# Moving part of VectorE's exponential onto GpSimd, beside chosen VectorE instructions, in a multi-query attention kernel

## Chip, cores and metric

The kernel runs on one core of a Trainium2 chip. The metric is the device time in microseconds (us); lower is better. PE is the matrix engine (PEld its weight loads), ACT the scalar engine, DVE the vector engine, POOL is GpSimd and SP the sync engine, which here only starts DMAs.

## The reference

```python
q: (8, 1024, 16, 64)   k, v: (8, 1024, 64)      # float32, one k and v for all 16 heads
scores  = q @ k.T / sqrt(64)                    # per batch and head, 1024 x 1024
weights = exp(scores - max); weights /= sum(weights)
out     = weights @ v
```

There are 8 x 16 x 1024 x 1024 = 134 million exponentials. They are the work that this kernel spreads over engines.

## The kernel before

Two heads form a pair; there are 64 pairs with 8 key tiles each, 512 "tiles" of 128 keys x 2 heads x 1024 queries. For each tile PE computes the scores in two halves (128 x 1024 values in PSUM each), and a weight tile in fp16 comes back from one of two engines:

- ACT computes exp directly: two ACTIVATEs of 128x1024 per tile.
- DVE takes some tiles by another road. It turns the score into the bits of an fp16 number (`z`, two instructions, one per half), cuts out the exponent (`e`), builds a mantissa (`m`), squares it and multiplies it by `z`. The sum of `e`, `z` and this product, each with its own scaled copy of v, is close to exp. So a DVE tile costs PE three value products where an ACT tile costs one.

```python
def exp_dve(t, c):                       # once per half of the tile; cut
    V.tensor_scalar(out=z[half c], in0=scores, scalar1=vscale, scalar2=..., op0=mult, op1=add)
    steps[t] = (                                                  # each on 128 x 2048
        lambda: V.tensor_scalar(out=e, in0=z, scalar1=0xFC00, op0=bitwise_and),
        lambda: V.tensor_scalar(out=m, in0=z, scalar1=1023, scalar2=14 << 10, and, or),
        lambda: V.tensor_tensor(out=m, in0=m, in1=m, op=mult),    # the square
        lambda: V.tensor_tensor(out=m, in0=z, in1=m, op=mult),    # the product
    )
```

A planner (`plan`) simulates PE, ACT and DVE with assumed durations before the kernel is built. It decides which tiles go to DVE and fixes the order of every instruction on every engine. Its constants, such as `ACT_P` (the assumed spacing of ACTIVATEs), are tuned. POOL only starts DMAs (loads of q and k). The accumulated output is normalised on DVE (`rec`, `norm`).

The softmax here doesn't subtract the row's maximum and nothing guards it: scores larger than these inputs give would overflow.

Of the kernel before, what the change touches and what calls it, by code (L numbers as in the profile page):

```python
# [10 lines left out]
FP16 = mybir.dt.float16  # L11
U16 = mybir.dt.uint16
EXP = mybir.ActivationFunctionType.Exp
ALU = mybir.AluOpType
ENG = mybir.EngineType

P = 128
ONE = 1024.0
C0 = 0.4578223016
TERMS = (1.0, 1.017578125, 0.66650390625)  # L20

ACT_P, ACT_L = 0.905, 1.19
QK_P, AV_B, AV_1, SWITCH, PE_L = 0.22, 0.0295, 0.02, 0.10, 0.49
MARGIN, WAIT = 0.285, 0.097
END, END_LAG = 4.686, 0.6
VEC = dict(z=1.13, rec=0.11, val=0.34)
NORM = 0.07, 0.067
STEPS = (0.6, 0.6, 1.13, 1.13)
VEC_L = 0.19
VEC_DEP = 0.12  # L30
BACKLOG, BACK_END = 7.741, 3.823
LAST, SPLIT, FIRST = 13, 6, 3
RAMP, VALS, COLD, WARM = 0.395, 3.0, 1, 0.0
BUSY = 20, 3, 5, 2
WBUFS = 23
ZBUFS = 6
LAG = 1.833
FAR = 1e9
BLOCKS = (0, 6, 10, 16)
STEP = 2  # L40

def follows(x, y):
    if y is None:
        return False
    if len(x) == 5:
        return len(y) == 5 and x[1] == "norm" and y[1] == "rec" and x[2:] == y[2:]
    if len(x) != 2 or len(y) != 2:
        return False
    if y[0] == "z":
        return x in ((y[1], 0), (y[1], 1))  # L50
    return x[0] == y[0] and (x[1], y[1]) in ((2, 1), (3, 2))

def plan(NP, NKT, HP=8):
# [8 lines left out]
    def emit(t, *op):  # L62
        ops.append((t, len(ops), op))

    pe = act = dve = 0.0
    mode = ""
    slot = [0.0] * 3
# [10 lines left out]
    p, g = 0, 0  # L78
    groups: list = []
    zs: list = []  # L80
    evs: list = []
    steps: list = []
    vals = [(VALS, 0, k) for k in range(len(TERMS))]
    vdone: dict = {}
    last = None
    while p < NP or groups:
        assert min(pe, dve) < 2e3
        if pe <= dve:
# [23 lines left out]
                units = [(t, c) for c in range(2) for t in range(nt, n)]  # L112
                nt = n
            if nt // NKT >= HP * nb - 3 and nb * HP < NP:
                vals += [(T, nb, k) for k in range(len(TERMS))]
                nb += 1
            cold = COLD if T < WARM else 1
            free = [s for s in range(3) if slot[s] <= T + (SWITCH if mode != "qk" else 0)]
# [88 lines left out]
                pe = max(min(nxt, default=0.0), T + 1e-3)  # L207
        else:
            T = dve
            z = [x for x in zs if x[0] <= T + 0.25]  # L210
            todo = [("ev", x) for x in evs if x[0] <= T]
            todo += [("val", x) for x in vals if x[0] <= T][:1]
# [4 lines left out]
            if z:  # L217
                x = z[0]
                zs.remove(x)
                r, s, u = x  # L220
                T = max(T, r)
                emit(T, "z", *u)
                dve = T + VEC["z"]
                slot[s] = dve + VEC_L
                if u[1] == 1:
                    steps += [(u[0], n) for n in range(len(STEPS))]
                    ready[u[0], 1, "v"] = dve + VEC_L
                last = ("z", u[0])
            elif what == "ev":
                evs.remove(x)  # L230
                emit(T + late, *x[1:])
                dve = T + late + vec(x[1], x[3])
                if x[1] == "rec":
                    evs.insert(0, (T, "norm", *x[2:]))
                else:
                    acc[x[4]] = dve + VEC_L
                last = x
            elif what == "val":
                vals.remove(x)
                emit(T, "val", *x[1:])  # L240
                dve = T + VEC["val"]
                vdone[x[1:]] = dve + VEC_L
                last = None
            elif what == "step":
                steps.remove(x)
                emit(T + late, "step", *x)
                dve = T + late + STEPS[x[1]]
                if x[1] in (0, len(STEPS) - 1):
                    ready[x[0], x[1] and len(TERMS) - 1, "v"] = dve + VEC_L
                last = x  # L250
            else:
                nxt = [x[0] for x in zs + evs + vals if x[0] > T] + [pe + 1e-6] * (pe > T)
                dve = max(min(nxt, default=0.0), T + 1e-3)
                last = None
    for x in evs:
# [6 lines left out]
def kernel(  # L262
# [47 lines left out]
    zs: dict = {}  # L310
    ms: dict = {}
    steps: dict = {}
    acc: dict = {}
    rec: dict = {}
    osb: dict = {}

    def load_k(b):
        st = kst.setdefault(b, {})
        st["k16"] = kvp.tile([P, NKT, 2, D], FP16, tag="k16", name=f"k16{b}")
        for r in range(2):  # L320
            nc.gpsimd.dma_start(  # L321
                out=st["k16"][:, :, r, :], in_=k[b].rearrange("(p c) d -> p c d", p=P)
            )
# [4 lines left out]
            st["vn"] = kvp.tile([P, NKT, D], FP32, tag="vn", bufs=1, name=f"vn{b}")  # L328
        nc.sync.dma_start(out=st["vn"], in_=v[b].rearrange("(p c) d -> p c d", p=P))

    def scale_v(b, k):
        kst[b]["v"] = vals[b % 2]
        nc.vector.tensor_scalar(  # L333
            out=vals[b % 2][k][:, :, 0:D], in0=kst[b]["vn"], scalar1=TERMS[k], scalar2=None,
            op0=ALU.mult)

# [117 lines left out]
    def exp_dve(t, c):  # L454
        name = f"{t}"
        if c == 0:
            zs[t] = dvp.tile([P, 2, S], U16, tag="z", bufs=ZBUFS, name=f"z{name}")
        z = zs[t]
        nc.vector.tensor_scalar(  # L459
            out=z[:, :, c * QC : (c + 1) * QC], in0=sc.pop((t, c)), scalar1=vscale,  # L460
            scalar2=(15 + math.log2(C0)) * ONE, op0=ALU.mult, op1=ALU.add,
        )
        if c == 0:
            return
        V = nc.vector
        m = ms[t] = dvp.tile([P, 2, S], FP16, tag="m", bufs=ZBUFS, name=f"m{name}")
        wt[t] = dvp.tile([P, 2, S], FP16, tag="e", bufs=ZBUFS, name=f"e{name}")
        steps[t] = (
            lambda: V.tensor_scalar(  # L469
                out=wt[t].bitcast(U16), in0=z, scalar1=0xFC00, scalar2=None,  # L470
                op0=ALU.bitwise_and),
            lambda: V.tensor_scalar(  # L472
                out=m.bitcast(U16), in0=z, scalar1=1023, scalar2=14 << 10,
                op0=ALU.bitwise_and, op1=ALU.bitwise_or),
            lambda: V.tensor_tensor(out=m, in0=m, in1=m, op=ALU.mult),  # L475
            lambda: V.tensor_tensor(out=m, in0=z.bitcast(FP16), in1=m, op=ALU.mult),  # L476
        )

    def value(p, grp, j, k, x, n, end, s):
        if n == 0:  # L480
# [16 lines left out]
    def reciprocal(p, grp):  # L497
        a = blocks(p, grp)
        rec[p, grp] = recp.tile([P, 8], FP32, tag="rec", name=f"rec{p}_{grp}")
        nc.vector.reciprocal(out=rec[p, grp][:, 0 : a.shape[1]], in_=a[:, :, D])  # L500

    def normalise(p, grp):
        b, hp = divmod(p, HP)
        a = blocks(p, grp)
        n = a.shape[1]
        if grp == 0:
            osb[p] = osbp.tile([P, NKT, 2 * D], FP32, tag="osb", name=f"osb{p}")
        o = osb[p]
        nc.vector.tensor_tensor(  # L509
            out=o.rearrange("p i (h d) -> p (i h) d", h=2)[:, BLOCKS[grp] : BLOCKS[grp + 1], :],  # L510
            in0=a[:, :, 0:D],
            in1=rec.pop((p, grp))[:, 0:n].unsqueeze(2).broadcast_to([P, n, D]),
            op=ALU.mult,
        )
        acc.pop((p, grp))
        if p == NP - 1:
            i0, i1 = BLOCKS[grp] // 2, BLOCKS[grp + 1] // 2
        elif grp == 2:
            i0, i1 = 0, NKT
        else:  # L520
            return
        (nc.scalar if p == NP - 1 and grp == 1 else nc.sync).dma_start(
            out=out[b, P * i0 : P * i1, 2 * hp : 2 * hp + 2, :].rearrange(
                "(c p) h d -> p c (h d)", p=P),
            in_=o[:, i0:i1, :],
        )

    begun = 0

    def begin(w):  # L530
        if w % 2 == 0:
            if w + 4 < NP:
                load_q(w + 4)
            if w + 2 < NP:
                trans_q(w + 2)
        b, hp = divmod(w, HP)
        if b + 1 < B:
            if hp == 2:
                load_k(b + 1)
            if hp == 4:  # L540
                load_v(b + 1)
            if hp == HP - 3:
                trans_k(b + 1)

    with tc.manual_schedule(engines={ENG.PE, ENG.Activation, ENG.DVE, ENG.Pool}):
# [7 lines left out]
        for _, _, (op, *args) in order:  # L553
            if op == "qk":
                if scores == 5:
                    turn_first(2)
                scores += 1
                while begun <= args[0] // NKT:
                    begin(begun)
                    begun += 1  # L560
                score(*args)
                if scores < 3:
                    busy(BUSY[3])
                if scores == 3:
                    turn_first(1)
            elif op == "act":
                exp_act(*args)
            elif op == "z":
                exp_dve(*args)
            elif op == "val":  # L570
                scale_v(*args)
            elif op == "step":
                steps[args[0]][args[1]]()
            elif op == "av":
                value(*args)
            elif op == "rec":
                reciprocal(*args[:2])
            else:
                normalise(*args[:2])

_INS = ['q', 'k', 'v']
_OUTS = [((8, 1024, 16, 64), 'float32')]
# [24 lines left out]
```

## Time and profile before

The median is 763.3 us (15 runs, 761.9 to 766.0). The page of the profiled run begins with the busy time of each engine and its number of instructions, and gives the chain of work that ended last:

```profile
span 761.6 us, 29604 instructions
PE 733.1 (96%) x13648; PEld 489.6 (64%) x13648; DVE 723.3 (95%) x1048; ACT 749.0 (98%) x816; POOL 43.6 (6%) x60
ACT 88%; PE 10%; DVE 1%; DMA 0%; issue 0%
```

Three engines are almost full. The chain goes through ACT for 88% of the span. The groups of instructions of the same page show what each one does (columns: line, engine, operation, output and input with shapes, count | total busy us, mean ns of one | idle time just before them and what ended it):

```profile
L448 ACT ACTIVATE w<-sc 128x1024 f16<-128x1024 f32 x814 | 747.1, 1323 | 4.3 <-PE sc L436 4.2
L459 DVE TENSOR_SCALAR z<-sc 128x1024 uint16<-128x1024 f32 x210 | 256.2, 1220 | 15.0 <-PE sc L436 12.2
L475 DVE TENSOR_TENSOR m<-m 128x2048 f16<-128x2048 f16 x105 | 126.9, 1209 | 0.1
L476 DVE TENSOR_TENSOR m<-z,m 128x2048 f16<-128x2048 f16 x105 | 126.4, 1204 | 0.0
L469 DVE TENSOR_SCALAR e<-z 128x2048 uint16<-128x2048 uint16 x105 | 72.8, 693 | 0.0
L472 DVE TENSOR_SCALAR m<-z 128x2048 uint16<-128x2048 uint16 x105 | 72.1, 686 | 0.0
L333 DVE TENSOR_SCALAR vals<-vn 128x512 f16<-128x512 f32 x24 | 9.1, 412 | 0.0
```

DVE holds 105 of the 512 tiles, ACT the other 407 (814 ACTIVATEs). ACTIVATEs overlap: a record lasts 1.32 us in the mean, but neighbours start 0.904 us apart at the least and 0.921 us in the mean. The train of 813 spacings lasts 748.6 us, so about 15 us of the time are outside it (start, tail, and what the span leaves out). ACT sat idle before scores for 4.2 us only.

The ends of the records: 804 of 813 ends follow the end before by 0.914 to 0.919 us, 0.917 in the middle.

### The profile page before, as it was taken

How to read it: one execution, taken by the hardware profiler on the slowest of the kernel's cores; microseconds unless marked ns; L12 is line 12 of the kernel's file. 1: busy time of each engine (PE TensorE's matmuls, PEld its weight loads, DVE VectorE, ACT ScalarE, POOL GpSimd, SP SyncE). 2: the span in 40 equal slices, each digit the busy share in tenths (PEclk: the TensorE clock that was granted, in tenths of full speed). 3: DMA queues.
4: the chain of work that ended last, by engine and by line, in shares of the span. 5: the costliest groups of instructions: out<-in, count | busy, mean ns of one | idle time of the engine just before them, and what ended most of it. 6: DMA issues, size and time to landing. Idle time of an engine off the chain costs nothing.

```text
span 761.6 us, 29604 instructions
## 1 busy us (share of the span) xinstructions
PE 733.1 (96%) x13648; PEld 489.6 (64%) x13648; DVE 723.3 (95%) x1048; ACT 749.0 (98%) x816; POOL 43.6 (6%) x60
## 2 busy tenths in 40 slices
PE   8899999999999999999999999999999999999997
PEld 5456566666666666666666666666665666666666
DVE  5999999999999999999999999999999999999982
ACT  6999999999999999999999999999999999999997
POOL 2100010000100001000010000100000000000000
PEclk8999999999999999999999999999999999999999
DMA  6973475354754538654585543746548545342313
GB/s 124 120 134 71 84 125 109 76 106 93 116 102 78 124 59 132 113 94 97 92 122 97 113 95 89 111 87 127 111 78 102 104 85 113 85 86 58 84 51 92
DMA packets 189980, 75.04 MB, mean 99 GB/s; under 512 B 90272, under 2 KB 188832, under 8 KB 189856
## 3 DMA queue, kind: packets, MB, share of 16 engines
q1 hardware_dynamic: 140544, 54.01, 31.4%
q0 software_dynamic: 47840, 18.35, 21.3%
q8 instruction: 106, 1.74, 0.9%
q10 hardware_dynamic: 1472, 0.79, 0.3%
q14 instruction: 18, 0.15, 0.1%
HBM read 39.58 MB, written 33.55 MB: 96 GB/s over the span
## 4 chain that ended last, share of the span: by engine, by line
ACT 88%; PE 10%; DVE 1%; DMA 0%; issue 0%
ACT w L448 88%; PE acc L487 6%; PE sc L436 4%; DMA kn<-in_k_dram 0%; DVE z L459 0%; PE busy L392 0%; PE kps L412 0%; DVE osb L509 0%; PE qps L423 0%; DVE k L407 0%; DVE qt L425 0%; DVE rec L500 0%
## 5 line engine op out<-in xcount | busy, mean ns | idle before, releaser
L448 ACT ACTIVATE w<-sc 128x1024 f16<-128x1024 f32 x814 | 747.1, 1323 | 4.3 <-PE sc L436 4.2
L436 PE MATMUL sc<-qt,k2t 64*128 64x512 f16 x2048 | 345.6, 384 | 21.6 <-ACT w L448 16.4
L487 PE MATMUL acc<-vals,w 128*128 128x65 f16 x6512 | 314.4, 194 | 0.2 <-DVE osb L509 0.2
L487 PEld LDWEIGHTS <-w 128*128 128x128 f16 x6512 | 241.0, 97 | 98.4 <-issue 97.4
L459 DVE TENSOR_SCALAR z<-sc 128x1024 uint16<-128x1024 f32 x210 | 256.2, 1220 | 15.0 <-PE sc L436 12.2
L436 PEld LDWEIGHTS <-k2t 64*128 64x128 f16 x2048 | 100.6, 93 | 96.6 <-issue 43.6
L475 DVE TENSOR_TENSOR m<-m 128x2048 f16<-128x2048 f16 x105 | 126.9, 1209 | 0.1
L476 DVE TENSOR_TENSOR m<-z,m 128x2048 f16<-128x2048 f16 x105 | 126.4, 1204 | 0.0
L487 PE MATMUL acc<-vals,e 128*128 128x65 f16 x1680 | 110.6, 194 | 0.6 <-DVE osb L509 0.6
L487 PE MATMUL acc<-vals,z 128*128 128x65 f16 x1680 | 109.9, 194 | 0.0
L487 PE MATMUL acc<-vals,m 128*128 128x65 f16 x1680 | 104.5, 194 | 0.4 <-issue 0.4
L509 DVE TENSOR_TENSOR osb<-acc,rec 128x384 f32<-128x384 f32 (+1 forms) x192 | 96.8, 506 | 0.4
L487 PEld LDWEIGHTS <-e 128*128 128x128 f16 x1680 | 74.1, 97 | 25.2 <-issue 23.3
L487 PEld LDWEIGHTS <-z 128*128 128x128 f16 x1680 | 74.1, 97 | 22.2 <-issue 22.2
L487 PEld LDWEIGHTS <-m 128*128 128x128 f16 x1680 | 71.7, 97 | 22.3 <-issue 21.6
L469 DVE TENSOR_SCALAR e<-z 128x2048 uint16<-128x2048 uint16 x105 | 72.8, 693 | 0.0
L472 DVE TENSOR_SCALAR m<-z 128x2048 uint16<-128x2048 uint16 x105 | 72.1, 686 | 0.0
L356 POOL DMA_DIRECT2D qn<-in_q_dram x32 | 29.1, 910 | 620.9 <-DMA qt<-qn 587.5
L500 DVE RECIPROCAL rec<-acc 128x6 f32<-128x6 f32 (+1 forms) x192 | 34.4, 181 | 12.5 <-PE acc L487 12.5
L321 POOL DMA_DIRECT2D k<-in_k_dram x14 | 13.0, 933 | 0.0
L333 DVE TENSOR_SCALAR vals<-vn 128x512 f16<-128x512 f32 x24 | 9.1, 412 | 0.0
L392 PE MATMUL busy<-ident 128*128 128x128 f16 x32 | 4.2, 303 | 1.6 <-POOL ident masks.py:199 1.6
(22 smaller groups left out, 13.7 us busy)
## 6 DMA issues: line engine op xcount, KB each, us to landing
out_dram<-osb SPq DMA_DIRECT2D x63, 512.0 KB, 3.4
qn<-in_q_dram POOLq DMA_DIRECT2D x31, 512.0 KB, 5.9
vn<-in_v_dram SPq DMA_DIRECT2D x8, 256.0 KB, 3.7
k<-in_k_dram POOLq DMA_DIRECT2D x14, 128.0 KB, 5.8
qf<-in_q_dram ACTq DMA_DIRECT2D x2, 256.0 KB, 3.7
qt<-qn SPq DMA_TRANSPOSE x32, 4.6
out_dram<-osb SPq DMA_DIRECT2D x2, 192.0 KB, 2.1
qn<-in_q_dram POOLq DMA_DIRECT2D x1, 256.0 KB, 5.3
```

Of the source, the lines that this page charges most:

```text
L321: nc.gpsimd.dma_start(out=st["k16"][:, :, r, :], in_=k[b].rearrange("(p c) d -> p c d", p=P))
L356: nc.gpsimd.dma_start(out=qn[ps[0]].rearrange("p (c r) x -> p c (r x)", r=len(ps)), in_=q[b, :, 2 * hp : 2 * hp + 2 * len(ps), :].rearrang ...
L436: nc.tensor.matmul(sc[t, c][:, h, :], kst[p // HP]["k2t"][64 * h : 64 * h + 64, j, :], qt[p][64 * h : 64 * h + 64, 4 * c : 4 * c + 4, :], ...
L448: ins = nc.scalar.activation(out=w, in_=sc.pop((t, c)), func=EXP, scale=ascale).ins
L459: nc.vector.tensor_scalar(out=z[:, :, c * QC : (c + 1) * QC], in0=sc.pop((t, c)), scalar1=vscale, scalar2=(15 + math.log2(C0)) * ONE, op0= ...
L469: lambda: V.tensor_scalar(out=wt[t].bitcast(U16), in0=z, scalar1=0xFC00, scalar2=None, op0=ALU.bitwise_and),
L472: lambda: V.tensor_scalar(out=m.bitcast(U16), in0=z, scalar1=1023, scalar2=14 << 10, op0=ALU.bitwise_and, op1=ALU.bitwise_or),
L475: lambda: V.tensor_tensor(out=m, in0=m, in1=m, op=ALU.mult),
L476: lambda: V.tensor_tensor(out=m, in0=z.bitcast(FP16), in1=m, op=ALU.mult),
L487: nc.tensor.matmul(acc[p, grp][:, o : o + D + 1], w[:, h, i * P : (i + 1) * P], kst[p // HP]["v"][k][:, j, 0 : D + 1], start=(n == 0 and y ...
L500: nc.vector.reciprocal(out=rec[p, grp][:, 0 : a.shape[1]], in_=a[:, :, D])
L509: nc.vector.tensor_tensor(out=o.rearrange("p i (h d) -> p (i h) d", h=2)[:, BLOCKS[grp] : BLOCKS[grp + 1], :], in0=a[:, :, 0:D], in1=rec.p ...
```

## The change

The intent is to relieve DVE, so that it can take more tiles and ACT fewer. Of the square, 896 of 2048 columns go to POOL in two pieces of 448, and so do 21 of the 24 scalings of v. POOL and DVE share SBUF ports, so each piece is placed in the plan beside a DVE instruction that reads PSUM (`z`, or `rec` for the scalings), with an extra dependence on the DVE instruction ahead of it. A piece that finds no such place within 9.1 us gets a gap of 0.7 us on DVE in the plan. DMA starts of POOL are held until after a piece. Many of the tuned constants changed too.

```diff
-ACT_P, ACT_L = 0.905, 1.19
+ACT_P, ACT_L = 0.917, 1.19
-MARGIN, WAIT = 0.285, 0.097
-END, END_LAG = 4.686, 0.6
+MARGIN, WAIT = 0.309, 0.061
+END, END_LAG = 8.479, 0.592
-STEPS = (0.6, 0.6, 1.13, 1.13)
+STEPS = (0.6, 0.6, 0.665, 1.13)
+PIECE, PIECE_T, PIECE_AGE, LATE = 448, 1.2, 9.124, 0.7
...                                                   (more constants)
+    def beside(t, age, kinds):                        # planner
+        x = next((x for x in pool if x[0] <= t - age and x[1] in kinds), None)
...
             elif z: ...
+                beside(T, 0.3, ("sq",))               # a square piece goes beside z
                 emit(T, "z", *u)
...
-            lambda: V.tensor_tensor(out=m, in0=m, in1=m, op=ALU.mult),
+            lambda: square(V, 0, 2 * S - 2 * PIECE),
...
+    def beside(op, t, n):                             # building the kernel
+        if op == "sq":
+            a = 2 * S - (2 - n) * PIECE
+            ins = squares[t](nc.gpsimd, a, a + PIECE)
+        else:
+            ins = scale_v(t, n, nc.gpsimd)
+        (before, y), (last, x) = past[-2:]
+        tc.add_manual_dep(ins.ins, (last if follows(x, y) else before).name, ...,
+            reason="shared SBUF ports")
+        while later:
+            later.pop(0)()                            # DMA starts that were held back
```

The built kernel has 110 DVE tiles, 804 ACTIVATEs and 160 more value matmuls (11,712 for 11,552).

More of the change, by code (lines that the diff above doesn't have):

```diff
@@ L20 @@
 TERMS = (1.0, 1.017578125, 0.66650390625)
-ACT_P, ACT_L = 0.905, 1.19
+ACT_P, ACT_L = 0.917, 1.19
 QK_P, AV_B, AV_1, SWITCH, PE_L = 0.22, 0.0295, 0.02, 0.10, 0.49
-MARGIN, WAIT = 0.285, 0.097
-END, END_LAG = 4.686, 0.6
+MARGIN, WAIT = 0.309, 0.061
+END, END_LAG = 8.479, 0.592
 VEC = dict(z=1.13, rec=0.11, val=0.34)
 NORM = 0.07, 0.067
-STEPS = (0.6, 0.6, 1.13, 1.13)
+STEPS = (0.6, 0.6, 0.665, 1.13)
+PIECE, PIECE_T, PIECE_AGE, LATE = 448, 1.2, 9.124, 0.7
 VEC_L = 0.19
 VEC_DEP = 0.12
-BACKLOG, BACK_END = 7.741, 3.823
-LAST, SPLIT, FIRST = 13, 6, 3
-RAMP, VALS, COLD, WARM = 0.395, 3.0, 1, 0.0
-BUSY = 20, 3, 5, 2
+BACKLOG, BACK_END = 7.606, 1.715
+LAST, SPLIT, FIRST = 14, 16, 3
+RAMP, VALS, COLD, WARM = 0.556, 3.0, 1, 0.0
+BUSY = 20, 3, 5, 0
 WBUFS = 23
 ZBUFS = 6
-LAG = 1.833
+LAG = 1.89
 FAR = 1e9
@@ L42, in follows @@
 def follows(x, y):
-    if y is None:
+    if x is None or y is None:
         return False
@@ L63, in emit @@
         ops.append((t, len(ops), op))
+    def beside(t, age, kinds):
+        x = next((x for x in pool if x[0] <= t - age and x[1] in kinds), None)
+        if x is None:
+            return False
+        pool.remove(x)
+        emit(t, *x[1:])
+        if x[1] == "val":
+            vdone[x[2:]] = t + PIECE_T
+        elif x[3] == 1:
+            squared.append((t + PIECE_T, x[2]))
+        return True
+    squared: list = []
     pe = act = dve = 0.0
@@ L82, in plan @@
     steps: list = []
+    pool: list = []
     vals = [(VALS, 0, k) for k in range(len(TERMS))]
@@ L114, in plan @@
             if nt // NKT >= HP * nb - 3 and nb * HP < NP:
-                vals += [(T, nb, k) for k in range(len(TERMS))]
+                pool += [(T, "val", nb, k) for k in range(len(TERMS))]
                 nb += 1
@@ L209, in plan @@
             T = dve
+            if beside(T, PIECE_AGE, ("sq", "val")):
+                T += LATE
+                dve = T
+            steps += [(x[1], len(STEPS) - 1) for x in squared if x[0] <= T]
+            squared = [x for x in squared if x[0] > T]
             z = [x for x in zs if x[0] <= T + 0.25]
@@ L225, in plan @@
                 if u[1] == 1:
-                    steps += [(u[0], n) for n in range(len(STEPS))]
+                    steps += [(u[0], n) for n in range(len(STEPS) - 1)]
                     ready[u[0], 1, "v"] = dve + VEC_L
@@ L230, in plan @@
                 evs.remove(x)
+                if x[1] == "rec":
+                    beside(T, 0.3, ("val",))
                 emit(T + late, *x[1:])
@@ L247, in plan @@
                 dve = T + late + STEPS[x[1]]
+                if x[1] == len(STEPS) - 2:
+                    pool += [(dve, "sq", x[0], n) for n in range(2)]
                 if x[1] in (0, len(STEPS) - 1):
@@ L251, in plan @@
             else:
-                nxt = [x[0] for x in zs + evs + vals if x[0] > T] + [pe + 1e-6] * (pe > T)
+                nxt = [x[0] for x in zs + evs + vals + squared if x[0] > T] + [pe + 1e-6] * (pe > T)
                 dve = max(min(nxt, default=0.0), T + 1e-3)
@@ L312 @@
     steps: dict = {}
+    squares: dict = {}
+    later: list = []
     acc: dict = {}
@@ L315, with load_k @@
     osb: dict = {}
-    def load_k(b):
+    def load_k(b, r):
         st = kst.setdefault(b, {})
-        st["k16"] = kvp.tile([P, NKT, 2, D], FP16, tag="k16", name=f"k16{b}")
-        for r in range(2):
+        if r == 0:
+            st["k16"] = kvp.tile([P, NKT, 2, D], FP16, tag="k16", name=f"k16{b}")
+        if True:
             nc.gpsimd.dma_start(
@@ L329, in load_v, with scale_v @@
         nc.sync.dma_start(out=st["vn"], in_=v[b].rearrange("(p c) d -> p c d", p=P))
-    def scale_v(b, k):
+    def scale_v(b, k, engine):
         kst[b]["v"] = vals[b % 2]
-        nc.vector.tensor_scalar(
+        return engine.tensor_scalar(
             out=vals[b % 2][k][:, :, 0:D], in0=kst[b]["vn"], scalar1=TERMS[k], scalar2=None,
@@ L458, in exp_dve @@
         z = zs[t]
-        nc.vector.tensor_scalar(
+        yield nc.vector.tensor_scalar(
             out=z[:, :, c * QC : (c + 1) * QC], in0=sc.pop((t, c)), scalar1=vscale,
@@ L467, in exp_dve, with square @@
         wt[t] = dvp.tile([P, 2, S], FP16, tag="e", bufs=ZBUFS, name=f"e{name}")
+        flat = m.rearrange("p h x -> p (h x)")
+        def square(engine, a, b):
+            return engine.tensor_tensor(
+                out=flat[:, a:b], in0=flat[:, a:b], in1=flat[:, a:b], op=ALU.mult)
+        squares[t] = square
         steps[t] = (
@@ L474, in exp_dve @@
                 op0=ALU.bitwise_and, op1=ALU.bitwise_or),
-            lambda: V.tensor_tensor(out=m, in0=m, in1=m, op=ALU.mult),
+            lambda: square(V, 0, 2 * S - 2 * PIECE),
             lambda: V.tensor_tensor(out=m, in0=z.bitcast(FP16), in1=m, op=ALU.mult),
         )
+    def beside(op, t, n):
[5 more added lines that the diff above has]
+        (before, y), (last, x) = past[-2:]
+        tc.add_manual_dep(
+            ins.ins, (last if follows(x, y) else before).name,
+            mybir.DependencyInfo(mybir.DependencyClass.Sync, mybir.DependencyReason.DATA),
+            reason="shared SBUF ports")
+        while later:
+            later.pop(0)()
     def value(p, grp, j, k, x, n, end, s):
@@ L499, in reciprocal @@
         rec[p, grp] = recp.tile([P, 8], FP32, tag="rec", name=f"rec{p}_{grp}")
-        nc.vector.reciprocal(out=rec[p, grp][:, 0 : a.shape[1]], in_=a[:, :, D])
+        yield nc.vector.reciprocal(out=rec[p, grp][:, 0 : a.shape[1]], in_=a[:, :, D])
     def normalise(p, grp):
@@ L508, in normalise @@
         o = osb[p]
-        nc.vector.tensor_tensor(
+        yield nc.vector.tensor_tensor(
             out=o.rearrange("p i (h d) -> p (i h) d", h=2)[:, BLOCKS[grp] : BLOCKS[grp + 1], :],
@@ L526, in normalise @@
         )
+    past: list = []
     begun = 0
@@ L532, in begin @@
             if w + 4 < NP:
-                load_q(w + 4)
+                later.append(lambda: load_q(w + 4))
             if w + 2 < NP:
@@ L537, in begin @@
         if b + 1 < B:
-            if hp == 2:
-                load_k(b + 1)
+            if hp in (1, 3):
+                later.append(lambda: load_k(b + 1, hp // 2))
             if hp == 4:
@@ L567 @@
                 exp_act(*args)
-            elif op == "z":
-                exp_dve(*args)
-            elif op == "val":
-                scale_v(*args)
-            elif op == "step":
-                steps[args[0]][args[1]]()
+            elif op == "sq" or op == "val" and args[0] > 0:
+                beside(op, *args)
             elif op == "av":
                 value(*args)
-            elif op == "rec":
-                reciprocal(*args[:2])
-            else:
-                normalise(*args[:2])
+            else:
+                if op == "z":
+                    done, key = exp_dve(*args), ("z", args[0])
+                elif op == "val":
+                    done, key = [scale_v(*args, nc.vector)], None
+                elif op == "step":
+                    done, key = [steps[args[0]][args[1]]()], tuple(args)
+                elif op == "rec":
+                    done, key = reciprocal(*args[:2]), ("", op, *args)
+                else:
+                    done, key = normalise(*args[:2]), ("", op, *args)
+                past.extend((x.ins, key) for x in done)
 _INS = ['q', 'k', 'v']
```

## The prediction

> **What bounds the kernel.** The page's busy table gives ACT 749.0 of 761.6 us (98%), PE 733.1, DVE 723.3, POOL 43.6. The chain of work that ended last is 88% the exp ACTIVATE, 6% value matmuls, 4% score matmuls. There are 814 ACTIVATEs. Starts of neighbours in the trace lie 0.904 us apart at the least, 0.917 typically, 0.921 in the mean; outside this train there are about 15 us. 763.6 = 813 x 0.921 + 15. PE is the second limit: in the stretches of 100 us it is 96 to 99% busy, and about half of the ACTIVATEs start within 60 ns of the end of their score matmuls. DVE is about as full (97 to 99%), which caps the number of key tiles whose exp it can take: 105 of 512.
>
> **What the change does.** From each DVE tile, 896 of the 2048 columns of the square (two pieces of 448) go to GpSimd, as do 21 of 24 scalings of v. Built order: 110 DVE tiles instead of 105, 804 ACTIVATEs instead of 814, 160 value matmuls more (11,712 for 11,552), 220 GpSimd pieces.
>
> Costs:
> - ACT: -10 ACTIVATEs x 0.92 = -9.2 us.
> - PE: +160 matmuls at about 30 ns (runs of 24 take 0.8 to 0.9 us) = +4.8 us.
> - DVE: the square shrinks from 1.209 us to about 0.74 (estimate, scaled from the 2048 form): -46 us; scalings of v -8.7; five more tiles at 5.0 us = +25. Net about 723 to 694: DVE gets some 60 us of slack, which is partly spent waiting for pieces.
> - GpSimd: estimate from the Trainium skill's "GPSIMD Engine Reference" (Performance versus the Vector engine: 4497 ns for 2048 fp32 two-input elements): about 1.0 to 1.2 us a piece, no trace shows it yet; 220 pieces = 220 to 260 us, POOL busy near 40%.
>
> **Contention.** The skill's page "SBUF — State Buffer" (Who interferes with whom) says GpSimd shares a port pair with DVE, held for a whole instruction, against DVE ops in two-port modes or with two SBUF inputs. The order puts 207 of 220 square pieces beside the z op (1.22 us), which reads PSUM and should not collide. No trace so far shows this. I expect few collisions: e and mask steps stay near 0.69 us in the mean, at most 0.85.
>
> **On the path.** Only the 10 ACTIVATEs shorten the chain; the DVE relief pays only through them. The new schedule is planned at ACT's typical 0.917 us, so ACT should rarely run dry, but PE gets 4.8 us more work in 9 us less: its idle time in the middle nearly vanishes. I expect a spacing of 0.918 to 0.924.
>
> **Time.** 803 x 0.921 + 15 = 754.5 us (-1.2%). Range 750.5 to 760. Chances: faster by over 2% 0.06, within 2% 0.88, slower 0.06.
>
> **What would show it.** Right: 804 ACTIVATEs, spacing near 0.92, ACT 98%; DVE near 695 us, POOL 250 to 320; PE over 97%. Wrong: ACT idle before PE scores of more than 10 us (PE bound), DVE means of the 4x steps or the product clearly longer (port lock), DVE idle waits on GpSimd ahead of the last product, or pieces above 1.3 us.
>
> **What could make it wrong.** Pieces longer than z, so that the lock stalls DVE and then PE; descriptor generation on GpSimd delayed so that queries come late; PE saturation, which would return the 9 us.

## More of the kernel before

The shortest ACTIVATE record is 1.017 us. A record is longer when the instruction's scores were ready early: it then begins while the one ahead still runs. In this run only 53 of 813 records (the first left out) are under 1.10 us, so ACT nearly always had its next input waiting.

## The result, and the profile after

The changed kernel takes 754.7 us (median of 9 runs, 754.3 to 757.7). Its ratio to the kernel before is 0.9893, with a 95% interval of 0.9881 to 0.9905. Ratios here are the mean time of one kernel's fast runs over that of the other's of the same rounds, so they are not quite the ratio of the medians. It is clearly faster, by 1.1%.

The same parts of the page after:

```profile
span 753.4 us, 30262 instructions
PE 729.0 (97%) x13804; PEld 483.0 (64%) x13804; DVE 707.6 (94%) x1057; ACT 741.2 (98%) x806; POOL 362.2 (48%) x301
ACT 57%; PE 29%; DVE 11%; issue 1%; POOL 1%; DMA 0%; DVEq 0%
```

```profile
L476 ACT ACTIVATE w<-sc 128x1024 f16<-128x1024 f32 x804 | 739.3, 1191 | 2.6 <-PE sc L464 2.3
L499 POOL TENSOR_TENSOR m<-m 128x448 f16<-128x448 f16 x220 | 283.3, 1290 | 358.5 <-DVE osb L558 82.2
L487 DVE TENSOR_SCALAR z<-sc 128x1024 uint16<-128x1024 f32 x220 | 268.3, 1219 | 17.5 <-PE sc L464 13.5
L511 DVE TENSOR_TENSOR m<-z,m 128x2048 f16<-128x2048 f16 x110 | 135.6, 1235 | 3.5 <-POOL m L499 3.5
L499 DVE TENSOR_TENSOR m<-m 128x1152 f16<-128x1152 f16 x110 | 82.1, 746 | 0.1
L504 DVE TENSOR_SCALAR e<-z 128x2048 uint16<-128x2048 uint16 x110 | 80.2, 729 | 0.9
L507 DVE TENSOR_SCALAR m<-z 128x2048 uint16<-128x2048 uint16 x110 | 76.5, 695 | 0.0
L361 POOL TENSOR_SCALAR vals<-vn 128x512 f16<-128x512 f32 x21 | 36.8, 1753 | 5.4 <-DVE m L511 2.1
```

*The sum of the gain.* The ACTIVATE train shrank from 813 spacings (748.6 us) to 803 (739.5 us), the first ACTIVATE starts at 6.5 us in both, and the tail after the last one's start grew from 6.5 to 7.4 us. That is -9.1 + 0.9 = -8.2 us, the whole difference of the spans (761.6 - 753.4 = 8.2). The mean spacing is 0.921 us in both.

*The spacing is the same because ACT still runs at its own pace, but now with hardly any reserve behind it.* 766 of 803 ACTIVATEs end 0.914 to 0.919 us after the one ahead, and ACT lost 3.8 us beyond 0.917 an ACTIVATE, as before (3.9). What changed is how early its inputs come. The share of ACT is 98% in both, but the chain now runs through ACT for 57% only. The mean ACTIVATE record fell from 1.323 to 1.191 us although the work of one is the same. 264 of 803 records are now under 1.10 us (53 of 813 before): their scores came just in time, and 230 of the 264 still ended at ACT's pace. So PE delivers later than it did. How near a second limit lies is a matter for experiments.

*The port pair at work.* Of the 220 pieces, 94 have a record of under 1.1 us; the shortest is 0.922 us. 64 have records of 1.5 to 2 us, and all of those overlap DVE's product. Here is such a place in the changed kernel, DVE first and then POOL (columns: start us, duration us, what):

```profile
300.79 1.22 DVE L511 TENSOR_TENSOR m<-z,m 128x2048 f16<-128x2048 f16 x1
302.61 1.22 DVE L487 TENSOR_SCALAR z<-sc 128x1024 uint16<-128x1024 f32 x1 [0.61 <-PE sc L464]
```

```profile
300.95 1.84 POOL L499 TENSOR_TENSOR m<-m 128x448 f16<-128x448 f16 x1 [0.96 <-DVE osb L558]
```

The product keeps its usual 1.22 us and ends at 302.0. The piece was let go at 300.95 and ends at 302.79, 0.79 us after the product. In all 67 such meetings the piece ends 0.78 to 0.80 us after the product, whenever it began. This fits a piece that stood blocked until the product gave up the shared ports and then ran for most of its 0.92 us. The Trainium skill's page "SBUF — State Buffer", section "Who interferes with whom", says the same: a DVE instruction with two SBUF inputs contends with a GpSimd instruction that reads SBUF, and whoever issues first gets the shared pair for the whole instruction. It is why the mean record of a piece, 1.29 us, is no measure of its work. Beside `z`, which reads PSUM, there is no contention: 203 of the 220 `z` records overlap a piece or a scaling by over 0.3 us and last 1.219 us in the mean, as they did before the change.

### The profile page after: what moved, and what is told of

Same layout as the page of the kernel before. It is cut to its first block, busy times and chain, and to the rows that moved or that the text cites. A ratio compares the mean times of both kernels' runs of the same rounds, so it can differ in the third digit from the quotient of the medians.

```text
span 753.4 us, 30262 instructions
## 1 busy us (share of the span) xinstructions
PE 729.0 (97%) x13804; PEld 483.0 (64%) x13804; DVE 707.6 (94%) x1057; ACT 741.2 (98%) x806; POOL 362.2 (48%) x301
## 4 chain that ended last, share of the span: by engine, by line
ACT 57%; PE 29%; DVE 11%; issue 1%; POOL 1%; DMA 0%; DVEq 0%
ACT w L476 57%; PE acc L536 17%; PE sc L464 11%; DVE z L487 4%; DVE m L511 2%; DVE m L499 1%; DVE m L507 1%; DVE osb L558 1%; DVE e L504 1%; POOL m L499 0%; DMA kn<-in_k_dram 0%; POOL vals L361 0%; DVE rec L549 0%; PE kps L440 0%; DVE qt L453 0%
## 5 line engine op out<-in xcount | busy, mean ns | idle before, releaser
L476 ACT ACTIVATE w<-sc 128x1024 f16<-128x1024 f32 x804 | 739.3, 1191 | 2.6 <-PE sc L464 2.3
L499 POOL TENSOR_TENSOR m<-m 128x448 f16<-128x448 f16 x220 | 283.3, 1290 | 358.5 <-DVE osb L558 82.2
L487 DVE TENSOR_SCALAR z<-sc 128x1024 uint16<-128x1024 f32 x220 | 268.3, 1219 | 17.5 <-PE sc L464 13.5
L511 DVE TENSOR_TENSOR m<-z,m 128x2048 f16<-128x2048 f16 x110 | 135.6, 1235 | 3.5 <-POOL m L499 3.5
L464 PEld LDWEIGHTS <-k2t 64*128 64x128 f16 x2048 | 88.5, 93 | 71.3 <-issue 26.8
L536 PE MATMUL acc<-vals,e 128*128 128x65 f16 x1760 | 123.8, 194 | 0.1
L536 PE MATMUL acc<-vals,z 128*128 128x65 f16 x1760 | 118.2, 194 | 0.0
L499 DVE TENSOR_TENSOR m<-m 128x1152 f16<-128x1152 f16 x110 | 82.1, 746 | 0.1
L504 DVE TENSOR_SCALAR e<-z 128x2048 uint16<-128x2048 uint16 x110 | 80.2, 729 | 0.9
L361 POOL TENSOR_SCALAR vals<-vn 128x512 f16<-128x512 f32 x21 | 36.8, 1753 | 5.4 <-DVE m L511 2.1
```

Of the source, the lines that this page charges most:

```text
L361: return engine.tensor_scalar(out=vals[b % 2][k][:, :, 0:D], in0=kst[b]["vn"], scalar1=TERMS[k], scalar2=None, op0=ALU.mult)
L464: nc.tensor.matmul(sc[t, c][:, h, :], kst[p // HP]["k2t"][64 * h : 64 * h + 64, j, :], qt[p][64 * h : 64 * h + 64, 4 * c : 4 * c + 4, :], ...
L476: ins = nc.scalar.activation(out=w, in_=sc.pop((t, c)), func=EXP, scale=ascale).ins
L487: yield nc.vector.tensor_scalar(out=z[:, :, c * QC : (c + 1) * QC], in0=sc.pop((t, c)), scalar1=vscale, scalar2=(15 + math.log2(C0)) * ONE ...
L499: return engine.tensor_tensor(out=flat[:, a:b], in0=flat[:, a:b], in1=flat[:, a:b], op=ALU.mult)
L504: lambda: V.tensor_scalar(out=wt[t].bitcast(U16), in0=z, scalar1=0xFC00, scalar2=None, op0=ALU.bitwise_and),
```

## The experiments

Theory A, that of the prediction: the gain is ten ACTIVATEs fewer, and relieving DVE is what makes room for that. Rival B: the retuned constants and order give the gain. Rival C: a relieved DVE steadies the pace, whatever the number of ACTIVATEs. A second question is how far behind ACT the next limit lies, before and after the change.

### The constants alone

```diff
 # kernel before
-ACT_P, ACT_L = 0.905, 1.19
+ACT_P, ACT_L = 0.917, 1.19
 # and MARGIN, WAIT, END, BACKLOG, LAST, SPLIT, RAMP, BUSY, LAG as in the change
```

> The kernel before with the new constants of the change and no GpSimd work: the planner then gives 104 tiles to DVE and 816 ACTIVATEs. Theory A (the gain is ten ACTIVATEs fewer, made possible by relieving DVE): about 816 x 0.921 + 14 = 765 us, no faster than before. Rival B (the gain is the retuned order of the engines): about 755 us, like the changed kernel.

Measured: 762.3 us, ratio to before 1.0014 (0.9993 to 1.0035). The planner left 104 tiles on DVE and 816 ACTIVATEs; their spacing is 0.921 us. The retuning alone gains nothing, so rival B falls as far as the constants go.

### The new order and the 110 tiles, with all of the work on DVE

```diff
 # changed kernel
-            lambda: square(V, 0, 2 * S - 2 * PIECE),
+            lambda: square(V, 0, 2 * S),
 # "sq" operations emit nothing; scalings of v run on nc.vector
```

> The changed kernel with its order and its 110 tiles, but the whole square and all scalings of v on DVE: DVE gets 110 x 0.46 + 8 = about 59 us more than in the changed kernel, where it sits idle for 46 us. Theory A: DVE becomes the limit, 770 to 795 us, and ACT idles before score matmuls. Rival B (the order alone gives the gain): about 755 us.

Measured: 785.1 us, ratio 1.0301 (1.0284 to 1.0319). The chain of its page:

```profile
span 784.2 us, 29935 instructions
DVE 69%; PE 26%; issue 4%; DMA 0%; DVEq 0%
```

DVE now sets the time. The order alone does not give the gain either. At 110 tiles in this order the work on GpSimd is worth 785.1 - 754.7 = 30.4 us; the kernel before had avoided this cost by giving DVE fewer tiles.

### GpSimd helps, but DVE gets only 105 tiles

```diff
 # changed kernel, planner
-                    not vunits and nt < NT - LAST and zfree
+                    not vunits and nt < NT - LAST and zfree
+                    and len(vring) < 104 * (nt + 8) / 500
```

> The changed kernel with the planner held to 105 tiles, so GpSimd still relieves DVE but ACT again has 814 ACTIVATEs. Theory A: 762 to 765 us, no better than before. Rival C (a relieved DVE makes the pace steadier and that is the gain): about 755 to 758 us.

Measured: 768.8 us (766.1 to 771.2), ratio 1.0089 (1.0056 to 1.0122). The kernel has 814 ACTIVATEs as before the change, and it is not faster than before, so it gives rival C no support. It came out slower than theory A said as well: in its profile, which is of one of the two quicker runs (766.7 us; the slower two, near 771, had a granted clock of 0.98 for 0.99), the mean spacing is 0.925 us, and ACTIVATEs lose 3.4 us to late starts between 600 and 650 us alone (the sum of spacings above 0.904), where the kernel before loses 0.6. The limit on the number of tiles made the planner choose another order, and that order is poorer. So the experiment shows only that offloading at 814 ACTIVATEs brought nothing in this order. What speaks against rival C more directly is the sum above: the mean spacing is 0.921 us with and without the change, so a steadier pace adds nothing to the gain. The experiment does not give the value of one ACTIVATE.

### The pieces without their place

```diff
 # changed kernel
-        (before, y), (last, x) = past[-2:]
-        tc.add_manual_dep(ins.ins, (last if follows(x, y) else before).name, ...,
-            reason="shared SBUF ports")
```

Data dependences still hold, so this is free of races. Only the moment at which a piece may start is different.

> The changed kernel without the extra dependence that ties each GpSimd piece to a DVE instruction, so a piece starts as soon as its mask step is done, mostly against DVE's own square, e and mask steps. Theory of the shared port pair: pieces and those DVE steps block each other, DVE means of e, mask and product rise well over 0.75 us and 1.24 us, 758 to 780 us. Rival (the pinning is a precaution that costs nothing to drop): 753 to 756 us, DVE means unchanged.

Measured: 808.8 us, ratio 1.0619 (1.0603 to 1.0636); 54 us slower than the changed kernel and 47 us slower than the kernel before in the same rounds. The same instructions do the same work. The groups and the chain:

```profile
DVE 66%; PE 30%; issue 3%; DMA 0%; DVEq 0%
L499 POOL TENSOR_TENSOR m<-m 128x448 f16<-128x448 f16 x220 | 271.3, 1247 | 419.5 <-DVE m L507 224.1
L511 DVE TENSOR_TENSOR m<-z,m 128x2048 f16<-128x2048 f16 x110 | 158.8, 1445 | 0.0
L499 DVE TENSOR_TENSOR m<-m 128x1152 f16<-128x1152 f16 x110 | 126.2, 1147 | 0.1
L504 DVE TENSOR_SCALAR e<-z 128x2048 uint16<-128x2048 uint16 x110 | 79.4, 722 | 0.9
```

The mask step of a tile releases the first piece and DVE's own part of the square at about the same time, so the two meet. DVE's square takes 1.147 us in the mean, where it took 0.746 us with pinned pieces; that alone is 44 us, nearly all that cutting the square had saved. The product takes 1.445 for 1.235 us, another 23 us. One meeting, two pieces on POOL first and then DVE:

```profile
298.98 1.82 POOL L499 TENSOR_TENSOR m<-m 128x448 f16<-128x448 f16 x2 [3.97 <-PE sc L464]
```

```profile
300.17 1.25 DVE L499 TENSOR_TENSOR m<-m 128x1152 f16<-128x1152 f16 x1
```

The second piece ends at 300.80 and the DVE square, which began at 300.17, ends at 301.42, 0.62 us later. Here DVE is the one that stood still. 78 squares began during a piece, and every one ended at least 0.61 us after that piece did, 72 of them within 0.61 to 0.63. The expected rise of the `e` step did not come (0.722 us, 0.729 in the changed kernel): only 5 `e` steps began during a piece.

### How much slack PE has

Every second tile computes 128 columns of its scores twice, which changes no result.

```diff
 # kernel before, and the same in the changed kernel; shortened
         sc[t, c] = psp.tile([P, 2, QC], FP32, ...)
+        if t % 2 == 0 and c == 0:
+            nc.tensor.matmul(sc[t, c][:, 0, 0:P], k2t[0:64, j, :], qt[p][0:64, 4 * c, :], ...)
```

> The kernel before with 256 idempotent extra score matmuls of 128 columns (one for the first half of every second key tile), an estimated 14 us of PE work. PE is idle for about 13.6 us between 100 and 700 us of the profile. Theory (PE is the second limit, close behind ACT): 3 to 8 us slower. Rival (PE has real slack behind its busy share): under 2 us slower.

> The changed kernel with the same 256 extra matmuls. PE is idle for about 9.4 us between 100 and 700 us. Theory (PE has still less slack after the change): 6 to 12 us slower than the changed kernel's 754.7, i.e. 761 to 767 us. Rival: under 2 us slower, 754 to 757 us.

Measured: the kernel before, 763.6 us, ratio 1.0007 (0.9981 to 1.0033), no change to be seen. The changed kernel, 761.6 us, 6.8 us more than without the extra work. Its PE busy time rose from 729.0 to 738.2 us, by 9.2; in the kernel before the same 256 matmuls raised it by 3.7 (736.8 for 733.1). So PE's busy time does not measure the added work, whose 14 us stay an estimate. So the expectation was wrong for the kernel before and right for the changed one. Before the change PE had room for this work; after it, PE has hardly any. In the changed kernel with the extra matmuls 644 of 803 ACTIVATE records are under 1.10 us, and ACT loses 8.9 us beyond its own pace, where the changed kernel loses 3.8: here PE does hold ACT up.

### A lighter ACT

Each ACTIVATE takes 960 of its 1024 columns. The result is wrong (the rest of each weight tile holds a constant, set once at the start by 46 memsets on GpSimd that the cut leaves out; they delay the first ACTIVATE from 6.5 to 8.4 us in both kernels).

```diff
-        w = wt[t][:, :, c * QC : (c + 1) * QC]
-        ins = nc.scalar.activation(out=w, in_=sc.pop((t, c)), func=EXP, scale=ascale).ins
+        w = wt[t][:, :, c * QC : c * QC + 480]
+        ins = nc.scalar.activation(out=w, in_=sc.pop((t, c))[:, :, 0:480], func=EXP, ...).ins
```

> Wrong result on purpose: each ACTIVATE of the kernel before takes 960 of its 1024 columns, 814 x 0.053 = 43 us less ACT work, all else in the same order. ACT alone the limit: about 720 us. Theory (PE close behind): only 8 to 20 us faster, 742 to 755 us.

> Wrong result on purpose: the same cut of each ACTIVATE in the changed kernel, 804 x 0.053 = 43 us less ACT work. ACT alone the limit: about 712 us. Theory (PE and DVE close behind, closer than before the change): only 4 to 14 us faster than 754.7, i.e. 740 to 751 us, so the changed kernel has little further to gain from ACT.

Measured: the kernel before falls to 750.1 us (ratio 0.9842), 12 us faster, as expected. Its chain no longer shows ACT as the limit:

```profile
PE 53%; DVE 42%; issue 3%; ACT 1%; DMA 0%
```

The changed kernel stays at 755.4 us (753.1 to 756.3). Its ratio to before is 0.9906 (0.9884 to 0.9928), against 0.9893 for the changed kernel with full ACTIVATEs. The expectation of 4 to 14 us missed: nothing was gained. ACT's own pace did become shorter: the ends of neighbours now lie 0.859 us apart at the least and most often 0.862 to 0.863, where it was 0.917 (0.054 less, for 0.053 expected). But only 367 of 803 keep within 0.859 to 0.866, and the mean spacing stayed at 0.920 us. Two lines of the lighter changed kernel's page say it, first the chain, then the busy time of the engines:

```profile
PE 65%; DVE 30%; issue 3%; POOL 1%; DMA 0%
PE 730.7 (97%) x13804; PEld 472.4 (63%) x13804; DVE 708.9 (94%) x1057; ACT 727.5 (97%) x806; POOL 367.0 (49%) x347
```

So a second limit, of PE and DVE, lies directly behind ACT in the changed kernel. With full ACTIVATEs their train takes 739.5 us, nearly all of it at ACT's own pace; with the lighter ones it takes 738.4 (the late start hides this 1 us in the time). In the kernel before, ACT was the limit, with the next one 12 us behind, or an estimated 14 without the late start. A share of 98% does not tell these cases apart, since it reads 97% here with 6% fewer columns and slack in ACT. The shortest record is 0.965 us here and starts lie 0.920 us apart in the mean, so the records overlap and leave hardly any idle time to see.

### A lighter ACT and a lighter PE

As above, with the score matmuls of ACT's tiles on 480 of 512 columns too (120 of each 128, the ACTIVATE likewise).

```diff
+        cut = P if t in vtiles else 120
             nc.tensor.matmul(
-                sc[t, c][:, h, :], ...
+                sc[t, c][:, h, :].rearrange("p (i x) -> p i x", x=P)[:, :, 0:cut], ...
```

> Wrong result on purpose: as act_light_before (each ACTIVATE on 960 columns, 750.1 us), and the score matmuls of the ACT tiles also on 480 of 512 columns, about 814 x 0.013 = 11 us less PE work. Theory (behind ACT the kernel before is held by DVE, 99.4% busy in the middle of act_light_before): within 3 us of 750. Rival (held by PE): about 740 us.

> Wrong result on purpose: the same two cuts in the changed kernel (ACT alone cut: 755.4 us, no gain). Theory (the changed kernel is held by PE): about 743 to 748 us. Rival (held by DVE or by waits for GpSimd pieces): 753 to 756 us.

Measured: before 745.5 us (4.6 less than with the lighter ACT alone), changed 749.4 us (6.0 less). The two clean theories, "held by PE" and "held by DVE", are both half wrong: of an estimated 11 us of PE work, the one returned 4.6 and the other 6.0. About 0.6 us of each comes from a start that is less late (7.8 us for 8.4), and the difference between the two is within the noise. With ACT light, PE work matters in the changed kernel where more ACT relief did not, so PE is on the chain of the second limit. But in these profiles PE waits for `z` to free score buffers and DVE waits for PE's scores, which suggests a loop of the two. The chain of the changed kernel in this last run:

```profile
PE 53%; DVE 43%; issue 3%; DMA 0%; POOL 0%
```

### Larger pieces

```diff
-            a = 2 * S - (2 - n) * PIECE
-            ins = squares[t](nc.gpsimd, a, a + PIECE)
+            a = 2 * S - (2 - n) * 640
+            ins = squares[t](nc.gpsimd, a, a + 640)
 # and DVE's square on 768 columns; same plan, same order
```

> The changed kernel in the same order with pieces of 640 columns and DVE's square of 768: DVE has about 22 us less to do, and a piece alone takes an estimated 1.3 us (0.93 us scaled by 640/448), longer than the z op of 1.22 us it stands beside. Shared port pair: the DVE op behind z collides, means of product and e rise, 756 to 768 us. Rival (PE alone sets the time, pieces of any size are free): 754 to 756 us.

Measured: 757.2 us (756.1 to 757.2), about 2.5 us slower than the changed kernel. DVE's busy time fell from 707.6 to 688.3 us, and that gained nothing. A still lighter DVE, by itself, is worth nothing in this order. It does loosen the second limit: only 73 of 803 ACTIVATE records are under 1.10 us (264 in the changed kernel), while ACT keeps its pace of 0.917 us in 782 intervals. The time agrees with the first theory but its mechanism does not show: the product takes 1.226 us (1.235 in the changed kernel) and `e` 0.744 (0.729). In the profile the loss lies in the first 50 us, where ACTIVATEs lose 5.1 us to late starts, against 2.6 in the changed kernel; after that it does slightly better. One profile each is too little to tell whether that start is systematic, so the cause of the 2.5 us stays open. An unblocked piece of 640 columns takes 1.242 us.

### A try for a faster plan

The planner's constants were searched for the shortest planned end at an assumed spacing of 0.907 us. The plan shortened from 739.7 to 732.2 us, with 109 tiles and pieces of 512 columns.

> A try for a faster kernel: the planner's constants searched for the shortest planned end at an ACT spacing of 0.907 us: 109 DVE tiles, pieces of 512 columns, 806 ACTIVATEs, 32 value matmuls fewer than the changed kernel; planned end 732 for 740. If the plan's PE durations hold on the chip: 746 to 751 us. If PE switches and port waits that the plan does not model decide: 753 to 760 us.

Measured: 756.0 us, ratio 0.9916 (0.9894 to 0.9938), and a wrong result (relative error 0.031). A replay of its planned order finds 12 tiles whose weight buffer is handed to a new tile before the last value matmul that reads it has been issued; the changed kernel has none. This fits the error but was not tested further. The result being wrong, the time shows only this: the plan's 7.5 us did not arrive. The trace points to ACT's assumed spacing and not to PE: 793 of 805 ACTIVATEs end 0.914 to 0.919 us after the one ahead, and 805 x 0.010 us, the distance from 0.907 to 0.917, makes an estimate of 8 us. The changed kernel was planned at 0.917.

## Why the prediction was right

The time was 754.7 us, for 754.5 predicted. Point by point:

- **Only the ACTIVATEs shorten the chain.** Right as a sum: 10 fewer x 0.921 us is -9.2, and the tail took back 0.9. The two undo runs do not contradict it: constants alone 762.3 us, offloading at 814 ACTIVATEs 768.8 us, the latter in a poorer order.
- **Spacing of 0.918 to 0.924 us.** Right (0.921), and for the reason given: "ACT should rarely run dry", and it lost 3.8 us beyond its own pace in the whole train. But the prediction did not work out where the second limit would come to lie. The lighter ACT gained 12 us before the change and none after it, so that limit is now about 1 us behind ACT. That it did not come to lie above ACT, and so eat the gain, was feared ("PE saturation") and not calculated: this part is luck.
- **PE as the second limit.** The prediction read PE as delivering with hardly any slack already before the change, from ACTIVATEs that start within 60 ns of their scores. That reading was wrong: the kernel before absorbed the extra matmuls (ratio 1.0007). A record that starts just after its scores can still overlap the ACTIVATE ahead by 0.4 us, so its input was early. After the change PE has hardly any slack, as the prediction feared: the same matmuls cost 6.8 us. The sum of 4.8 us more PE work can't be checked by busy time, which fell from 733.1 to 729.0 us; and PE's idle time between 100 and 700 us fell from 13.6 to 9.4 us, so it did not nearly vanish.
- **DVE near 695 us.** Too low: 707.6. The square and the scalings saved about what was expected (-44.8 us with the five more tiles counted, and -8.0), but the sum took the other steps at their old durations. `e` takes 0.729 for 0.693 us and the product 1.235 for 1.204, together 7 us, about half of the miss. Port waits are the likely cause: `e` records that overlap a piece or a scaling by over 0.3 us last 0.819 us in the mean, those that overlap none 0.700. `e` stayed below the 0.85 us that the prediction allowed.
- **POOL 250 to 320 us, pieces 1.0 to 1.2 us.** The records say 362 us and 1.29 us. The work is shorter than estimated (0.92 us unblocked) and the records longer, since a piece that is let go early waits in its record. The 21 scalings, 1.75 us each, had no estimate.
- **Contention.** The claim that `z` and a piece do not disturb each other holds (`z` takes 1.219 us in the changed kernel, 1.220 before). The prediction's "4x steps" are `e` and the mask step. The danger named, that the lock stalls DVE and then PE, is real: without the placing it costs 54 us.

What stays open: how PE and DVE share the second limit, and what the ACTIVATEs lose in the first 50 us of each kernel.

## What to carry to other kernels

Work moved to GpSimd paid here through the ten ACTIVATEs that it let ScalarE drop, and only with each piece beside VectorE instructions that leave the shared ports alone; the place of the pieces was worth 54 us and the whole gain 8.6. A busy share of 98% does not say which engine sets the time: take a little work away from one engine and add a little to another, before and after the change, and see whether the time moves. Read an engine's own pace from the ends of its records before saying that another one holds it up. When a tuned kernel is rebalanced, expect to meet the second limit, and count the gain only up to there.

## What the Trainium skill lacked or had wrong

- "GPSIMD Engine Reference", "Performance versus the Vector engine", has measured two-input times for fp32 of 2048 elements only (4497 ns). Scaled to 448 columns that is 984 ns; the runs show 0.922 us for an unblocked fp16 square of 448 columns, both inputs the same, and 1.242 us for 640. It lacks a fixed part and a rate for this form; these two give an estimate of 1.7 ns a column and about 0.18 us, below the 2.2 ns an element that 4497 ns make. The shortest piece of 512 columns, 1.028 us, lies on the same line.
- The same page's engine table ("When to use GPSIMD", "Engine selection") calls one-input work "roughly line-rate". The scaling of v, fp32 to fp16, 512 elements a partition into rows of 66, took at least 1.484 us on GpSimd, against 0.42 us for the same instruction on VectorE.
- "SBUF — State Buffer", "Who interferes with whom", states the lock as these runs show it for the pieces, in both directions. It lacks what it costs in a stream of instructions: VectorE's square rose from 0.746 to 1.147 us in the mean when pieces were not placed. It also does not say that a blocked GpSimd instruction's record contains its wait (1.84 us for 0.92 us of work).
- The same section lets the first one keep the pair for the whole instruction. The records of the scalings do not look so: in the changed kernel 8 `e` steps and 6 squares of VectorE began during a scaling, and all ended before its record did, `e` by 0.46 us and the square by 0.22 to 0.27, while behind a piece `e` ended 0.55 us after it. Whether the ports or the record end at another moment is not shown.
- "ScalarE: Activation LUTs", "What ACT_TABLE_LOAD costs", gives 186 ns + 0.833 ns a column for the cheaper form of an ACTIVATE (immediate operands) and an overlap of about 93 ns, which makes an estimate of 0.946 us from one to the next for 1024 columns. The pace here, scores in PSUM to weights in SBUF, is shorter: 0.917 us between ends (most often 0.862 to 0.863 for 960 columns), and the shortest record is 1.017 us.
- No page that was read says that a longer ACTIVATE record is a sign of inputs that came early, or that the ends of the records show the engine's pace: the mean record was 1.323 us in the kernel before and 1.060 us in the changed kernel with extra matmuls, for the same work, while ends lie 0.917 us apart in the middle in both.
